# First stage of a hybrid token mixer: modulation as plain fp32 products, scale applied as a row, positions added by DMA

## Chip, cores and metric

One core of one Trainium2 chip runs the whole program. The metric is the device time of one execution in microseconds; the median of three runs stands for a kernel.

## What is computed

The reference is one layer of a diffusion backbone: 2048 latent tokens and 256 context tokens, 1024 wide. What matters here is its front part and the residual stream:

```python
x = x + grid_pos_embed(ROWS)                  # (2048, 1024): 512 columns by grid row, 512 by grid column
c_act, cctx_act = silu(c), silu(c_ctx)
mod_lat = c_act @ ada_w + ada_b               # six pieces of 1024: sh1, sc1, g1, sh2, sc2, g2
mod_ctx = cctx_act @ ada_w + ada_b
h_ctx = rmsnorm(ctx, norm1_g) * (1 + csc1) + csh1
h_lat = rmsnorm(x, norm1_g) * (1 + sc1) + sh1
y_ctx, states = token_mixers(h_ctx @ w_in, ...)
y_lat, _ = token_mixers(h_lat @ w_in, ..., states)
x = x + g1 * (y_lat @ w_out)
x = x + g2 * (relu(modulate(rmsnorm(x, norm2_g), sh2, sc2) @ w1) ** 2 @ w2)
return rmsnorm(x, final_g)
```

## The kernel before

Large products are made in three fp32r passes: an operand is split into a rounded part ("h" or "hi") and the rest ("l" or "lo"), and hi·h, hi·l and lo·h are added in psum. TensorE's instructions stand in the order in which the program issues them; those of the other engines are ordered by a scheduler, by priorities, and each engine and each DMA queue then works in order.

The first stage is the part that matters.

- **Modulation** (lines 264 to 298). The first 2048 columns of `ada_w` come in 32 tiles `aw` of 128x512, through eight buffers, on SP's queue. ScalarE rounds each to `awh`, VectorE or GpSimd subtracts to `awl`, and TensorE adds two products per tile into four psum banks `mps`; the stationary side is `csp`, silu(c) and silu(c_ctx) split in the same way. The four rows are copied out, transposed into a column layout (line 287) and become `mT` (shift and scale with the bias) and `sc1` (gain times one plus scale), one value per channel and per stream.
- **norm_in** (240 to 254), for each tile of 128 tokens: `xt` (four buffers) is loaded; for a latent tile `add_pos` loads `prow` in two DMAs and GpSimd adds `prow` and `posc` to the two halves of `xt` (237, 238). ScalarE squares with an accumulator (251), `rstd_of` makes the reciprocal root on ScalarE and VectorE with one Newton step (215 to 225), and VectorE scales `xt` by it (253). Four tiles are prepared ahead (two of context, two latent ones), and later ones two tiles ahead.
- **modulate** (436 to 452): TensorE transposes `xt` in two halves of four 128x128 blocks into psum `tp0` (four buffers). Each block is multiplied by `sc1` and shifted by `mT`, five of eight on VectorE (448), three on ScalarE (450), into `hy` (three buffers). ScalarE rounds to `hTh` (451), VectorE (first half) or GpSimd (second half) subtracts to `hTl` (452).
- **first(g)** (427): when a token group is complete, two column blocks of `w_in` are multiplied with it; these products are fed in between the tiles, 2.7 us of them a tile (`Filler`). Groups are 0 (context, 256 tokens, two tiles) and 1 to 4 (512 latent tokens, four tiles each). Line 462 then needs the products of group 4, and the other projections follow without a gap.

The output projection (`w_out`, 1253) loads x again, tile by tile, and calls `add_pos` a second time before the residual sum. `load_wo` brings a second copy of `posc` for it.

```python
r0, r1 = rstd_of(nrm, ss, 1, D, "n1")
nc.vector.tensor_scalar(xt, xt, r0, r1, op0=ALU.mult, op1=ALU.mult)
...
if k < 2 + hf:
    nc.vector.tensor_scalar(y[:, k, :], tp[:, k, :], sc1[:, kk, s:s + 1], mT[:, kk, s:s + 1], op0=ALU.mult, op1=ALU.add)
else:
    nc.scalar.activation(y[:, k, :], tp[:, k, :], AF.Identity, scale=sc1[:, kk, s:s + 1], bias=mT[:, kk, s:s + 1])
```

## Time and profile before

| | |
|---|---|
| median of three runs | 2805.06 us (2803.17 to 2809.77) |
| profiled execution | 2810.26 us |
| its span | 2808.50 us |
| mean granted clock of TensorE | 0.958 |
| busy share of the span | TensorE 91%, VectorE 63%, ScalarE 41%, GpSimd 35% |
| DMA, mean over the span | 178 GB/s |

The profile is of one execution. PE is TensorE (PEld its weight loads, which overlap the products), DVE VectorE, ACT ScalarE, POOL GpSimd, SP SyncE; a letter q behind a name is the engine's instruction queue, where DMAs are issued. Times of rows count from the start of the span. In a row of the order of time "x8" means that eight like instructions are merged, and the bracket gives the engine's idle time before them with what ended it. Shares over the whole span mix stages with different limits; the first stage is some 138 us of it.

### The profile page before, as it was taken

Reading aid. Unit: us, or ns where it says so; the run is one execution under the profiler, and the core shown is the slowest. Engines: PE = TensorE matmul, PEld = TensorE weight load, DVE = VectorE, ACT = ScalarE, POOL = GpSimd, SP = SyncE. Lnnn points to the kernel's source line nnn. Section 1 sums busy time; section 2 is a strip of 40 time slices with the busy share of each in tenths; the row PEclk is TensorE's granted clock in tenths of the full one; section 3 lists DMA queues with packets and bytes.
Section 4 is the critical chain, followed back from the end, with each engine's and each line's share of the span. In section 5 each row is a group of like instructions: output and inputs, shape, how many; then the busy total and the mean of one; then the engine's idle time right before and its main releaser. Section 6 shows DMA issues by size and latency. Waiting matters only on the chain. (4 is left out here: it accounts for less than half of the span.)

```text
span 2808.5 us, 36451 instructions
## 1 busy us (share of the span) xinstructions
PE 2559.5 (91%) x12239; PEld 2084.5 (74%) x12239; DVE 1775.4 (63%) x3041; ACT 1162.4 (41%) x2039; POOL 986.9 (35%) x868
## 2 busy tenths in 40 slices
PE   6798889899998888889996999989997999999997
PEld 3576667788887667777775888778885888878876
DVE  7955476156647886646657777766664275565576
ACT  6745421233335656433324444544444333222343
POOL 5724411245444443324444333333431222222211
PEclk7999989999999999889998999999998999999999
DMA  7443355666556665856754776655556576776564
GB/s 221 144 132 109 96 160 161 159 158 161 152 158 171 187 180 168 277 169 207 230 175 127 200 213 200 175 162 156 144 154 203 165 250 196 233 248 211 156 196 150
DMA packets 496455, 499.44 MB, mean 178 GB/s; under 512 B 88578, under 2 KB 371932, under 8 KB 496268
## 3 DMA queue, kind: packets, MB, share of 16 engines
q1 hardware_dynamic: 470316, 469.77, 55.6%
q10 hardware_dynamic: 20480, 15.73, 1.7%
q0 software_dynamic: 5472, 11.60, 1.5%
q8 instruction: 97, 1.59, 0.2%
q14 instruction: 90, 0.74, 0.1%
HBM read 345.27 MB, written 151.72 MB: 177 GB/s over the span
## 5 line engine op out<-in xcount | busy, mean ns | idle before, releaser
L365 PE MATMUL pp<-hTh,whi 128*128 128x512 f32 (+1 forms) x1048 | 435.1, 415 | 15.7 <-DVE evt L505 12.1
L367 PE MATMUL pp<-hTh,wlo 128*128 128x512 f32 (+1 forms) x1048 | 409.2, 390 | 2.2 <-POOL wlo L313 2.0
L366 PE MATMUL pp<-hTl,whi 128*128 128x512 f32 (+1 forms) x1048 | 407.3, 389 | 0.2 <-DVE hTl L452 0.2
L1714 PE MATMUL yps<-bh,ah 128*128 128x512 f32 x896 | 351.9, 393 | 17.5 <-ACT bh L1629 17.1
L1716 PE MATMUL yps<-bh,al 128*128 128x512 f32 x896 | 352.4, 393 | 12.0 <-DVE al L1421 11.2
L1715 PE MATMUL yps<-bl,ah 128*128 128x512 f32 x896 | 351.4, 392 | 0.5 <-DVE bl L1421 0.5
L1421 POOL TENSOR_TENSOR al<-ar,ah 128x1024 fp32r<-128x1024 f32 x56 | 141.8, 2531 | 504.3 <-ACT ah L1643 504.3
L1643 ACT CAST ah<-ar 128x1024 fp32r<-128x1024 f32 x112 | 117.9, 1053 | 359.0 <-PE yps L1715 313.3
L365 PEld LDWEIGHTS pp<-hTh,whi 128*128 128x128 f32 x1048 | 205.7, 196 | 53.4 <-DVE evt L505 14.0
L367 PEld LDWEIGHTS pp<-hTh,wlo 128*128 128x128 f32 x1048 | 204.0, 195 | 45.8 <-POOL wlo L313 3.7
L366 PEld LDWEIGHTS pp<-hTl,whi 128*128 128x128 f32 x1048 | 205.7, 196 | 35.5 <-issue 1.9
L1714 PEld LDWEIGHTS yps<-bh,ah 128*128 128x128 f32 x896 | 170.0, 190 | 53.5 <-ACT bh L1629 17.6
L1716 PEld LDWEIGHTS yps<-bh,al 128*128 128x128 f32 x896 | 169.9, 190 | 50.6 <-DVE al L1421 13.2
L1715 PEld LDWEIGHTS yps<-bl,ah 128*128 128x128 f32 x896 | 170.0, 190 | 36.6 <-DVE bl L1421 1.0
L1424 POOL TENSOR_TENSOR uz<-tz 128x512 f32<-128x512 f32 x32 | 50.3, 1572 | 387.1 <-ACT whi L1455 273.5
L1464 PE MATMUL accy<-th,wlo 128*128 128x512 f32 x384 | 151.2, 394 | 1.3 <-DVE wlo L1421 1.3
L1462 PE MATMUL accy<-th,whi 128*128 128x512 f32 x384 | 150.5, 392 | 1.7 <-DVE tz L1424 1.7
L1463 PE MATMUL accy<-tl,whi 128*128 128x512 f32 x384 | 150.3, 391 | 0.0
L1421 DVE TENSOR_TENSOR wlo<-wab,whi 128x512 fp32r<-128x512 f32 x128 | 117.1, 916 | 42.8 <-ACT whi L1455 42.8
L1421 DVE TENSOR_TENSOR wlo<-ws,whi 128x512 fp32r<-128x512 f32 x96 | 84.4, 879 | 92.0 <-ACT whi L1455 91.8
L1455 ACT CAST whi<-wab 128x512 fp32r<-128x512 f32 x128 | 79.2, 619 | 135.6 <-PE accy L1463 56.4
L1627 DVE TENSOR_TENSOR braw<-braw 128x1024 f32<-128x1024 f32 x56 | 75.0, 1339 | 72.5 <-DMA braw<-in_mlp_w_dram 69.6
(384 smaller groups left out, 5959.0 us busy)
## 6 DMA issues: line engine op xcount, KB each, us to landing
uD<-uz SPq DMA_DIRECT2D x224, 256.0 KB
ar<-uD SPq DMA_DIRECT2D x112, 512.0 KB
braw<-in_mlp_w_dram SPq DMA_DIRECT2D x112, 512.0 KB
wab<-in_mlp_w_dram SPq DMA_DIRECT2D x64, 512.0 KB
maw<-in_ada_w_dram SPq DMA_DIRECT2D x64, 256.0 KB
wraw<-in_w_in_dram SPq DMA_DIRECT2D x54, 256.0 KB
rb<-rD SPq DMA_DIRECT2D x96, 128.0 KB
aw<-in_ada_w_dram SPq DMA_DIRECT2D x32, 256.0 KB
```

The source lines that it names most:

```text
L365: nc.tensor.matmul(acc[:, 0:n], hi, hTh[g][:, k, :], start=k == 0, stop=False)
L366: nc.tensor.matmul(acc[:, 0:n], hi, hTl[g][:, k, :], start=False, stop=False)
L367: nc.tensor.matmul(acc[:, 0:n], lo, hTh[g][:, k, :], start=False, stop=k == KC - 1)
L1421: eng.tensor_tensor(o, a, b, op=ALU.subtract)
L1455: nc.scalar.copy(hi, w)
L1462: nc.tensor.matmul(acc, hi[:, k, :], T2[i][0][:, k, :], start=first and k == 0, stop=False, skip_group_check=True)
L1463: nc.tensor.matmul(acc, hi[:, k, :], T2[i][1][:, k, :], start=False, stop=False, skip_group_check=True)
L1464: nc.tensor.matmul(acc, lo[:, k, :], T2[i][0][:, k, :], start=False, stop=k == 3, skip_group_check=True)
L1643: nc.scalar.copy(hi, r_)
L1714: nc.tensor.matmul(acc, ah[:, p_, :], bh, start=p_ == 0, stop=False)
L1715: nc.tensor.matmul(acc, ah[:, p_, :], bl, start=False, stop=False)
L1716: nc.tensor.matmul(acc, al[:, p_, :], bh, start=False, stop=p_ == 7)
```

## The change

The modulation is no longer split: TensorE multiplies `cact` (silu of both streams, fp32) with the raw `aw` tile, one product instead of two, with no cast and no subtraction (line 265 now).

For latent tiles the scale is applied before the transposes. The two scale rows of the modulation are turned into one row of 1024 values (one plus bias plus scale, times the gain, lines 283 and 284), two products with a row of ones spread it over the partitions (289) and the copies of these make `scB`. `norm_in` then leaves a latent `xt` unscaled and hands on the reciprocal root `r0`; `modulate` makes `xt * r0 * scB` in one instruction (441) before the transposes, and one sum per half adds the shift behind them (449). Context tiles keep the old way. All `hTl` subtractions go to GpSimd (458).

The positions are a full 2048x1024 table in DRAM; `add_pos` is now one DMA per tile on GpSimd's queue that adds the table's rows to `xt` in place, in the first stage (16 of 512 KB) and in the output projection (16). `posc`, `prow`, the 64 loads of `prow` and the 64 GpSimd sums are gone.

```diff
-    csp = const.tile([P, KC, 4], F32R, name="csp")
...
-    def add_pos(pool, posc, i, xt, bufs=2):
-        prow = pool.tile([P, 512], F32, name="prow", bufs=bufs)
-        for hf in range(2):
-            nc.sync.dma_start(prow[64 * hf:64 * hf + 64, :], I["pos_r"][2 * i + hf:2 * i + hf + 1, :].to_broadcast([64, 512]))
-        nc.gpsimd.tensor_tensor(xt[:, 0:512], xt[:, 0:512], prow, op=ALU.add)
-        nc.gpsimd.tensor_tensor(xt[:, 512:1024], xt[:, 512:1024], posc, op=ALU.add)
+    def add_pos(i, xt):
+        nc.gpsimd.dma_start(xt, I["pos"][i * P:(i + 1) * P, :], accum_op=ALU.add)
...
-        nc.vector.tensor_scalar(xt, xt, r0, r1, op0=ALU.mult, op1=ALU.mult)
-        return xt
+        if g == 0:
+            nc.vector.tensor_scalar(xt, xt, r0, r1, op0=ALU.mult, op1=ALU.mult)
+            return xt, None
+        nc.vector.tensor_tensor(r0, r0, r1, op=ALU.mult)
+        return xt, r0
...
-                ah = adp.tile([P, 512], F32R, name="awh", bufs=3)
-                al = adp.tile([P, 512], F32R, name="awl", bufs=3)
-                nc.scalar.copy(ah, aw)
-                (nc.gpsimd if i % 5 in (0, 2) else nc.vector).tensor_tensor(al, aw, ah.bitcast(F32), op=ALU.subtract)
-            nc.tensor.matmul(mps[j][0:4, :], csp[:, k, :], ah, start=k == 0, stop=False)
-            nc.tensor.matmul(mps[j][0:2, :], csp[:, k, 0:2], al, start=False, stop=k == KC - 1)
+            nc.tensor.matmul(mps[j][0:2, :], cact[:, k, :], aw, start=k == 0, stop=k == KC - 1)
...
-    for j in range(4):
-        mrow = adp.tile([4, 512], F32, name="mrow", bufs=2)
-        (nc.vector.tensor_copy if j % 2 else nc.scalar.copy)(mrow, mps[j][0:4, :])
+    for j in (2, 3, 0, 1):
+        mrow = adp.tile([2, 512], F32, name="mrow", bufs=4)
+        (nc.vector.tensor_copy if j % 2 else nc.scalar.copy)(mrow, mps[j][0:2, :])
+        if j >= 2:
+            js = slice(512 * j - D, 512 * j - D + 512)
+            nc.vector.scalar_tensor_tensor(arow[:, js], arow[:, js], 1.0, mrow[0:1, :], op0=ALU.add, op1=ALU.add)
+            nc.vector.tensor_tensor(arow[:, js], arow[:, js], nrow[:, js], op=ALU.mult)
...
+    for hf in range(2):
+        sb = pp()
+        nc.tensor.matmul(sb, ones1, arow[:, 512 * hf:512 * hf + 512])
+        (nc.vector.tensor_copy if hf else nc.scalar.copy)(scB[:, 512 * hf:512 * hf + 512], sb)
...
+        if g:
+            nc.vector.scalar_tensor_tensor(xt, xt, rs, scB, op0=ALU.mult, op1=ALU.mult)
...
+            if g:
+                nc.vector.tensor_tensor(y, tp, mT[:, ks, 0:1].to_broadcast([P, 4, P]), op=ALU.add)
...
-            (nc.gpsimd if hf else nc.vector).tensor_tensor(hTl[g][:, ks, ts_], y, hTh[g][:, ks, ts_].bitcast(F32), op=ALU.subtract)
+            nc.gpsimd.tensor_tensor(hTl[g][:, ks, ts_], y, hTh[g][:, ks, ts_].bitcast(F32), op=ALU.subtract)
```

The change also moves instructions. On TensorE, behind the modulation (`mrow` are the modulation's rows, `tp` the transposed halves, the first two those of context tile 0), before:

```order
L279 MATMUL tr<-ident,pr 128x128
L287 MATMUL tr<-ident,mrow 128x4 x16
L444 MATMUL tp_551<-ident,xt 128x128 x4
L444 MATMUL tp_563<-ident,xt 128x128 x4
```

and now:

```order
L267 MATMUL tr<-ident,pr 128x128
L286 MATMUL tr<-ident,mrow 128x2 x16
L289 MATMUL pp<-row_287,row_288 128x512 x2
L447 MATMUL tp_394<-ident,xt 128x128 x4
L447 MATMUL tp_406<-ident,xt 128x128 x4
```

The two spreading products (`row_287` is the row of scales, `row_288` the ones) stand between the modulation's transposes and the context tiles.

On VectorE, at the same place (`ss_162` and `ss_181` are the squares of latent tiles 0 and 1, `tp0_551` to `tp0_587` the context halves), before:

```order
L448 TENSOR_SCALAR hy_552<-tp0_551,sc1_494,mT_491 128x128
L225 TENSOR_SCALAR n1t_151<-n1t_151 128x1
L448 TENSOR_SCALAR hy_552<-tp0_551,sc1_494,mT_491 128x128
L253 TENSOR_SCALAR xt_141<-xt_141,n1r_146,n1t_151 128x1024
L448 TENSOR_SCALAR hy_564<-tp0_563,sc1_494,mT_491 128x128 x3
L452 TENSOR_TENSOR hTl0_87<-hy_552,hTh0_86 128x4x128
L448 TENSOR_SCALAR hy_576<-tp0_575,sc1_494,mT_491 128x128 x2
L448 TENSOR_SCALAR hy_588<-tp0_587,sc1_494,mT_491 128x128 x3
L218 TENSOR_SCALAR n1v_168<-ss_162 128x1
```

and now (`ss_153` and `ss_168` are the squares of latent tiles 0 and 1, `row10241_287` the row of scales):

```order
L216 TENSOR_SCALAR n1v_159<-ss_153 128x1
L283 SCALAR_TENSOR_TENSOR row10241_287<-row10241_287,mrow_294 1x512
L219 SCALAR_TENSOR_TENSOR n1t_161<-n1r_156,n1v_159 128x1
L284 TENSOR_TENSOR row10241_287<-row10241_287,row10240_286 1x512
L223 TENSOR_SCALAR n1t_161<-n1t_161 128x1
L283 SCALAR_TENSOR_TENSOR row10241_287<-row10241_287,mrow_302 1x512
L216 TENSOR_SCALAR n1v_174<-ss_168 128x1
L247 TENSOR_TENSOR n1r_156<-n1r_156,n1t_161 128x1
L284 TENSOR_TENSOR row10241_287<-row10241_287,row10240_286 1x512
```

The variances of latent tiles 0 and 1 now stand ahead of the last instruction that makes the row of scales, and the context tiles' pieces come later.

Those pieces stand in the next stretch of VectorE (`tp0_394` to `tp0_431` belong to the context tiles, `xt_150`, `xt_165` and `xt_442` are latent tiles 0, 1 and 2):

```order
L290 COPY scB_293<-pp_325 128x512
L454 TENSOR_SCALAR hy_395<-tp0_394,sc1_337,mT_335 128x128 x2
L454 TENSOR_SCALAR hy_407<-tp0_406,sc1_337,mT_335 128x128 x3
L454 TENSOR_SCALAR hy_419<-tp0_418,sc1_337,mT_335 128x128 x2
L441 SCALAR_TENSOR_TENSOR xt_150<-xt_150,n1r_156,scB_293 128x1024
L441 SCALAR_TENSOR_TENSOR xt_165<-xt_165,n1r_171,scB_293 128x1024
L216 TENSOR_SCALAR n1v_451<-ss_445 128x1
L219 SCALAR_TENSOR_TENSOR n1t_453<-n1r_448,n1v_451 128x1
L223 TENSOR_SCALAR n1t_453<-n1t_453 128x1
L247 TENSOR_TENSOR n1r_448<-n1r_448,n1t_453 128x1
L441 SCALAR_TENSOR_TENSOR xt_442<-xt_442,n1r_448,scB_293 128x1024
L454 TENSOR_SCALAR hy_431<-tp0_430,sc1_337,mT_335 128x128 x3
```

The last half of the second context tile comes behind the variance and the scaling of latent tile 2, whose buffer `xt` is that of context tile 0.

## Rows read from the trace of the kernel before

**Rows 1.** Stretches of the span: length, then each engine's busy us (instructions), clock, DMA, GB/s.

```profile
100.00:130.00 30.00, 23.73 (x127) 19.30 (x126) 28.73 (x65) 24.35 (x60) 24.59 (x20) 1.00 0.43 139
140.00:160.00 20.00, 20.00 (x101) 16.86 (x100) 8.57 (x17) 6.78 (x12) 6.35 (x12) 1.00 0.55 152
```

**Rows 2.** Order of time, TensorE (start, us, engine, line, operation): transposes; last group's first product.

```profile
38.48 1.94 PE L444 MATMUL tp<-ident,xt 128*128 128x128 f32 x8 [2.54 <-DVE n1v L218]
...
64.09 1.94 PE L444 MATMUL tp<-ident,xt 128*128 128x128 f32 x8 [3.56 <-DVE xt L253]
...
130.84 1.07 PE L444 MATMUL tp<-ident,xt 128*128 128x128 f32 x8
...
137.62 0.50 PE L365 MATMUL pp<-hTh,whi 128*128 128x512 f32 x1 [1.52 <-ACT hTh L451]
```

**Rows 3.** Order of time, modulation: weight loads, first cast, two products, the last product.

```profile
1.92 24.66 SPq L271 DMA_DIRECT2D aw<-in_ada_w_dram  x32
...
4.63 1.27 ACT L274 CAST awh<-aw 128x512 fp32r<-128x512 f32 x2 [0.85 <-DMA aw<-in_ada_w_dram]
...
10.69 0.63 PE L277 MATMUL m<-awl,csp 128*2 128x512 f32 x1
...
12.50 0.39 PE L276 MATMUL m<-awh,csp 128*4 128x512 f32 x1
...
32.75 0.40 PE L277 MATMUL m<-awl,csp 128*2 128x512 f32 x1
```

**Rows 4.** Order of time, weight loads (PEld) of the mixer's fp32 gate products.

```profile
169.36 3.06 PEld L574 LDWEIGHTS qk<-xc,gw 128*128 128x128 f32 x8 [3.73 <-issue]
...
234.02 0.19 PEld L574 LDWEIGHTS qk<-xc,gw 128*128 128x128 f32 x1 [0.24 <-issue]
234.45 0.19 PEld L574 LDWEIGHTS qk<-xc,gw 128*128 128x128 f32 x1 [0.24 <-issue]
```

**Rows 5.** Order of time: issue of the first x loads, first use of one.

```profile
32.58 0.90 SPq L247 DMA_DIRECT2D xt<-in_x_dram  x2
...
38.03 2.71 POOL L238 TENSOR_TENSOR xt<-xt,posc 128x512 f32<-128x512 f32 x2 [5.89 <-DMA xt<-in_x_dram]
```

**Rows 6.** GpSimd's DMAs by tile: landing of lr (192 KB); issue and landing of bU (256 KB).

```profile
DMA to landing us min/median/max: 2.4/3.5/5.1
...
L1182 POOL DMA_DIRECT2D bU<-vbD x12: 754/772/795, 1103.0 to 1245.8; - x12
...
DMA to landing us min/median/max: 4.0/5.5/7.4
```

**Rows 7.** Groups of ScalarE, 33 to 150 us (busy us, mean ns of one | idle before).

```profile
L251 ACT ACTIVATE junk<-xt 128x1024 bf16<-128x1024 f32 x18 | 19.0, 1056 | 6.8 <-POOL xt L237 6.7
```

**Rows 8.** Stretch 45 to 57 us, instructions on whi alone (the first weights).

```profile
45.00:57.00 12.00, 2.13 (x7) 1.96 (x8) 5.20 (x8) 0.00 (x0) 0.00 (x0) 0.50 0.79 216
```

**Rows 9.** Groups of VectorE, 33 to 150 us.

```profile
L448 DVE TENSOR_SCALAR hy<-tp,sc,mT 128x128 f32<-128x128 f32 x90 | 32.6, 402 | 3.2 <-PE tp L444 2.2
L253 DVE TENSOR_SCALAR xt<-xt,n1r,n1t 128x1024 f32<-128x1024 f32 x18 | 22.1, 1229 | 0.8 <-DVE n1t L225 0.3
L452 DVE TENSOR_TENSOR hTl<-hy,hTh 128x512 fp32r<-128x512 f32 x18 | 21.1, 1170 | 1.3 <-ACT hTh L451 1.2
L221 DVE SCALAR_TENSOR_TENSOR n1t<-n1r,n1v 128x1 f32<-128x1 f32 x18 | 9.5, 528 | 1.6 <-ACT n1r L216 1.3
```

**Rows 10.** Groups of VectorE, whole span: a sum from psum, a sum of two SBUF tiles.

```profile
L1249 DVE TENSOR_TENSOR yg<-tr,ga 128x512 f32<-128x512 f32 x26 | 17.8, 684 | 0.3 <-PE tr L1247 0.3
...
L1627 DVE TENSOR_TENSOR braw<-braw 128x1024 f32<-128x1024 f32 x56 | 75.0, 1339 | 72.5 <-DMA braw<-in_mlp_w_dram 69.6 <-issue 2.3
```

**Rows 11.** Groups of GpSimd, 33 to 150 us.

```profile
L452 POOL TENSOR_TENSOR hTl<-hy,hTh 128x512 fp32r<-128x512 f32 x18 | 25.7, 1428 | 23.5 <-ACT hTh L451 14.5 <-DVE hy L448 6.0 <-issue 2.8
```

**Rows 12.** Waits, 1190 to 1480 us (total, times, longest).

```profile
PE pp L1266 <- POOL yl L1251: 6.8, 9, 1.5
```

**Rows 13.** Order of time, VectorE: two casts of the first weights.

```profile
52.41 1.83 DVE L312 CAST whi<-wraw 128x512 fp32r<-128x512 f32 x2
```

More of the change, by code (lines that the diff above doesn't have):

```diff
@@ L50, in consts @@
     pos_c = np.concatenate([np.sin(ac), np.cos(ac)], -1).astype(np.float32)
-    pos_c = np.concatenate([pos_c, pos_c], 0)
+    pos = np.concatenate([np.repeat(pos_r, GRID_W, 0), np.tile(pos_c, (rows, 1))], 1)
+    pos = np.ascontiguousarray(pos.astype(np.float32))
     s = np.arange(P)[:, None]
@@ L247, in norm_in @@
             nc.sync.dma_start(xt, x[i * P:(i + 1) * P, :])
-            add_pos(nrm, posc, i, xt)
+            add_pos(i, xt)
         ss = nrm.tile([P, 1], F32, name="ss", bufs=3)
@@ L456, in body @@
             xts[tiles[i + 2]] = norm_in(*tiles[i + 2])
-        modulate(g, j, xts.pop((g, j)))
+        modulate(g, j, *xts.pop((g, j)))
         if g and j == 1:
@@ L1215, in load_wo @@
                 yield
-        wo["pos"] = op_.tile([P, 512], F32, name="posc2")
-        nc.sync.dma_start(wo["pos"], I["pos_c"])
+        wo["ready"] = True
     def y_in(i):
@@ L1258, in w_out @@
             nc.sync.dma_start(x2s[i], x[i * P:(i + 1) * P, :])
-            add_pos(wo["op"], wo["pos"], i, x2s[i], 1)
+            add_pos(i, x2s[i])
         x2 = x2s[i]
@@ L1329, in out_proj @@
         yield from until(0)
-        while "pos" not in wo:
+        while "ready" not in wo:
             yield None
```

37 lines of the change are left out of this document (18 added, 19 removed).

## The prediction

> **What bounds the kernel now.** I read the table of stretches first. Behind the first stage TensorE is dense: 20.00 us busy of the 20 us from 140 to 160 [rows 1]. So the stage delays everything by as much as it lasts, and each us that it ends earlier or later is taken as one us of the kernel. I set the stage's end where the first product of the last token group starts, 137.62 us, which waits for ScalarE's last hTh [rows 2].
>
> The order of time shows three parts. Until 33.15 us the modulation is computed [rows 3]. Then come the context tiles (transposes from 38.48) and the first latent ones; the transposes of latent tile 2 (counted from 0) start at 64.09 and those of tile 15 at 130.84 [rows 2], so 13 tiles take 66.75 us, 5.13 each. In that steady part, from 100 to 130 (5.85 tiles), VectorE is busy 28.73 of 30 us, GpSimd 24.59, ScalarE 24.35, TensorE 23.73 at full granted clock [rows 1]. VectorE sets the pace with 4.9 us a tile, but the others stand close: 4.20, 4.16 and 4.06. Little can be won before the next one binds.
>
> **The modulation.** Removed are 32 ScalarE casts, 32 subtractions and one of two products a tile. What is left is a plain fp32 product of 128x512 for each of 32 weight tiles. The gate products of the mixer are such products: each shows as two loads and two passes, 0.43 us from load to load at 2.4 GHz [rows 4], so 0.86 a product; at 1.2 GHz the eight loads of products half as wide take 3.06 us, so 1.53 for a whole one. The small products of before take 0.63 us at 10.69 and 0.39 at 12.50 [rows 3]: the first stands for 1.2 GHz, the second for 2.4. The first weight tile is there at 4.63 [rows 3]. With 32 products at 0.86 the end is 32.2, with the slow rate until 11.1 it is 35.0; I take 34.5 against 33.15. TensorE, now the slower side, frees the eight weight buffers: the last load goes out after product 24, at 27.6, against 26.6 (1.92+24.66 [rows 3]). Everything behind it on SP's queue is about 1 us later, less the posc and prow loads that are gone.
>
> **The start of the tiles.** Here the change adds waits. VectorE's row of scales now has, ahead of its last multiply, the variance of latent tile 1; TensorE's two broadcast products wait for that multiply, and the context transposes are queued behind them, as the order in the section on the change shows. So the context tiles wait for latent tile 1's positions to have been added by DMA.
> - The x loads: before, issued at 32.58, the first was used at 38.03, when it landed [rows 5]. Now 38.5, the second 40.0.
> - The adding DMA, 512 KB issued by GpSimd: no row shows one. GpSimd's plain DMAs land 3.5 us after issue (192 KB, 2.4 to 5.1) and 5.5 (256 KB, 4.0 to 7.4) [rows 6]. The lower bound is 3.3, the fastest 192 KB row plus the missing 320 KB at the weights' rate (8.4 MB in 24.66 us, 340 GB/s); the upper is 10, the slowest 256 KB row plus 0.8 for the other half and 1.6 for reading what it adds to, rounded up. I take 5.0, the fast row plus 1.0 us of data and 1.6 for that second reading, nearest to the 5.5 for half the size. Landed: 43.5 and 45.0.
> - The square (1.06 [rows 7], with its accumulator 1.25), the variance (0.15) and the multiply (0.7) end at 47.1. Two fp32 broadcasts at 1.2 GHz, TensorE having idled, take 3.1: 50.2. Two tiles of context transposes at 1.94 [rows 2]: 54.2.
> - VectorE first makes the eight operands of the first weights, 5.20 us [rows 8], to 52.8, then half of scB, seven context pieces at 0.40 [rows 9] and two scalings of a latent tile, to 59.0.
> - Then it stands at tile 2's variance. That tile's buffer is free at 52.3; load 3.5, adding DMA 5.0, square 1.25, rest 1.3: 63.4, scaling done 64.7. Only then comes the last context half, and with it the psum buffer for tile 1's last half, ahead of 30 products of 256 columns (6.4 us). The transposes of tile 2 start at 73.3: **9.2 us later than before.**
>
> **The steady part.** VectorE loses, a tile, five affine pieces of 0.402, the scaling of 1.229 and the subtraction of 1.170 [rows 9]. It gains a scaling by a row, with two inputs from SBUF, a 128x1 product and two sums from psum. The sums cost 0.684 [rows 10]. The scaling's bounds are 1.25, what the square takes for the same elements, and 2.3, the 1.339 of a 128x1024 sum of two SBUF tiles [rows 10], stretched as the subtraction is to 1.170 from the 0.684 that a sum of its size takes; I take 1.5, near the 1.339, since GpSimd reads less than before. With the small ones (0.53 [rows 9], twice 0.15, 0.35 for the new one) and 0.34 of evacuations: 4.4 us. By the same sum of durations the tile of before has 5.56, of which 4.9 show as busy, since short ones overlap; so 3.9 to 4.4. GpSimd loses the two position sums and takes over the other subtraction: two at 1.43 [rows 11], 0.35 of memsets, and the issue of the DMA (a 256 KB one 0.77 [rows 6]; I take 1.0): 4.2 us, with waits for x in between. The row-wise loop of one buffer of four (load 3.5, DMA 5.0, square to scaling 4, transposes 1) is 13.5 us, 3.4 a tile, and does not bind. ScalarE only loses work. TensorE's 4.06 is the floor. I take **4.3 us a tile** between 4.06 and 5.2 (VectorE with the stretched scaling).
>
> **The sum.** VectorE has the sums of tiles 0 and 1 behind it at 68.7 and the scaling of tile 3 at 72.5. Left are the sums of tiles 2 and 3 (2.8) and 12 tiles at 4.3 (51.6): 126.9; idle time as in 100 to 130 (1.27 of 30) adds 2.3, the last cast 0.6: 129.8. That is 7.8 us before 137.62. In the output projection the 16 pairs of position sums go and 16 adding DMAs come. They lie beside TensorE's work: all its waits for GpSimd's yl are 6.8 us [rows 12], and the DMA waits for x where the sum waited. I take 0, with bounds of 2 us less and 4 more. The profiled run took 2810.26 us, of which the span is 2808.50; it lies 5.2 above the median of 2805.06. The sum makes 2802.5 of it, and **2797** of the median.
>
> On GpSimd's DMAs two rules of the Trainium skill speak. The page "DMA: Bandwidth & Descriptors" (Anatomy of one DMA, SWDGE path) fits about 2.0 us plus the bytes at 436 GB/s, an estimate of 3.2 us for these; the rows' 5.5 for 256 KB lie above it, and the short rival is that case. "SBUF — State Buffer" (Who interferes with whom) says that a VectorE copy, cast or scalar operation in its two-port mode keeps GpSimd from writing descriptors; the weight casts stand where the adding DMAs of tiles 0 to 2 are issued, and by one such cast pair (1.83 us [rows 13]) the sum would be 2799 instead of 2797. No row of before has such a DMA beside such a cast.
>
> **The rivals.**
> - **A short landing.** With 3.3 us, each of the two waits of the start is 1.7 shorter, and with TensorE's floor of 4.06 the stage ends at 123: 14 us saved, 2791. For it: the fast end of [rows 6]. Against it: x is added, not only written, while the small pieces of the first weights still move.
> - **No difference.** VectorE's scaling collides with GpSimd's two subtractions and a tile costs 4.8 to 5.1: 12 tiles take 6 to 10 us more than forecast and pay back no more than the start lost, 2803 to 2807. For it: the subtraction's 1.170 against 0.684 shows what such a collision costs.
> - **Slower, the landing chain.** The DMA's landing L enters the start twice and the loop of four tiles once, (8.5+L)/4 a tile, which passes 4.3 from 8.7 us on. With L=9 the stage ends at 138.7, with 10 at 143.7; from there the kernel is slower by 0.2%, and 11 gives about 2816. For it: 7.4 us already for 256 KB without adding. Against it: the medians.
> - **The fp32 products don't get the fast clock.** 32 at 1.53 end at 54 instead of 34.5, 19 us later, about 2816. Against it: TensorE is less idle than in the loop of before, which did get it.
>
> **How the numbers follow.** Forecast, 6 to 10 us saved: 0.31. Short landing: 0.17. No difference: 0.28. Landing chain 0.20, slow clock 0.04. A measurement of this kernel can tell about 0.2%, 5.6 us, from no change: faster 0.48, same 0.28, slower 0.24. The range leaves out a twentieth below and some 0.12 above: 2788 is the short landing with 2 us from the projection, 2812 a landing a little over 10 us.
>
> **What would show it.** One product row a weight tile, and the last about 34.5; the context transposes at 50 to 52 behind the two broadcasts, with VectorE waiting for ScalarE's square ahead of them; tile 2's transposes near 73; GpSimd's DMA rows with a landing near 5 us; then 4.3 us from tile to tile and the granted clock full from 80 on. I am wrong if tile 2 comes before 66 or after 80, if tiles still need 5 us, or if TensorE behind the stage waits where it did not.

## The result, and the profile after

The changed kernel took **2825.93 us** (median of four runs; 2822.88 to 2828.76), the kernel before on the same chip 2805.60 (2803.17 to 2809.77). The ratio, here and below estimated from all runs and not from the two medians, is 1.0070, 95% interval 1.0051 to 1.0090: **slower by 0.7%**, where 2797 had been forecast. The profiled run took 2828.76 us, its span is 2827.0 (before 2810.26 and 2808.5), so 18.5 us of span are to be found.

Stretches of the kernel after; columns as in [rows 1]:

```profile
100.00:130.00 30.00, 22.38 (x110) 18.73 (x111) 21.57 (x40) 14.86 (x33) 17.71 (x15) 0.83 0.85 187
```

Against [rows 1] every engine has become *less* busy: VectorE 21.57 of 30 us instead of 28.73, GpSimd 17.71 instead of 24.59. Yet fewer tiles get through. What rose is the DMA share, from 0.43 to 0.85. No engine sets the pace any more.

TensorE in the order of time, after; this answers to [rows 2] and the last of [rows 3] (the first row covers 13 products and ends at 35.28):

```profile
29.54 5.74 PE L265 MATMUL m<-aw,cact 128*2 128x512 f32 x13
...
36.34 1.13 PE L286 MATMUL tr<-ident,mrow 2*128 2x2 f32 x16 [0.80 <-DVE prm L268]
48.62 2.07 PE L289 MATMUL pp<-row,row 1*128 1x512 f32 x2 [11.15 <-DVE n1t L223]
51.79 2.07 PE L289 MATMUL pp<-row,row 1*128 1x512 f32 x2 [1.10 <-DVE row L284]
53.80 1.54 PE L447 MATMUL tp<-ident,xt 128*128 128x128 f32 x6
...
76.50 1.03 PE L447 MATMUL tp<-ident,xt 128*128 128x128 f32 x8
...
150.37 1.03 PE L447 MATMUL tp<-ident,xt 128*128 128x128 f32 x8
```

The modulation ends where it was forecast. Then TensorE stands for 11.15 us in front of the broadcasts of the scale row, the context transposes start at 53.80 (before 38.48, forecast 50.2), tile 2's at 76.50 (before 64.09), tile 15's at 150.37 (before 130.84). Thirteen tiles take 73.87 us, **5.68 each**; before 5.13, forecast 4.3.

The adding DMAs of the first stage, GpSimd's tile xt (durations of the issue in ns, then landing in us):

```profile
L229 POOL DMA_DIRECT2D xt<-in_pos_dram x16: 801/856/1207, 39.7 to 138.6; - x16
...
DMA to landing us min/median/max: 5.2/6.6/9.1
```

They land after 6.6 us in the median, where 5.0 was taken. ScalarE's groups, 33 to 165 us, show who waits for them (beside [rows 7]):

```profile
L242 ACT ACTIVATE junk<-xt 128x1024 bf16<-128x1024 f32 x18 | 19.0, 1056 | 42.4 <-DMA xt<-in_pos_dram 41.9 <-DMA xt<-in_ctx_dram 0.5
```

VectorE's groups, 80 to 140 us, beside [rows 9] and [rows 10]:

```profile
L441 DVE SCALAR_TENSOR_TENSOR xt<-xt,n1r,scB 128x1024 f32<-128x1024 f32 x11 | 17.1, 1556 | 0.4
L449 DVE TENSOR_TENSOR hy<-tp,mT 128x512 f32<-128x512 f32 x21 | 14.2, 686 | 1.0 <-PE tp L447 0.7
L247 DVE TENSOR_TENSOR n1r<-n1r,n1t 128x1 f32<-128x1 f32 x10 | 7.7, 773 | 0.3
L219 DVE SCALAR_TENSOR_TENSOR n1t<-n1r,n1v 128x1 f32<-128x1 f32 x10 | 6.7, 666 | 1.8 <-ACT n1r L214 1.7
```

The scaling (1556) and the sums (686) are near the 1.5 and 0.684 us assumed. Two products of a *single column* cost 773 and 666 ns.

**Where the 18.5 us are.** Six landmarks of both traces, in us of the span; each is the start of an instruction, the end excepted. Their differences are not evenly spread, and one of them is negative:

| landmark | before | after | difference |
|---|---|---|---|
| ScalarE's last cast hTh of the stage | 138.30 | 155.12 | +16.8 |
| first qk product of L1155 (after: L1161), in the mixer's last part | 1116.8 | 1133.2 | +16.4 |
| first product of the output projection (yl) | 1238.7 | 1243.2 | +4.5 |
| first product of the MLP's accy | 1492.4 | 1498.2 | +5.8 |
| last product of accy | 2144.6 | 2159.7 | +15.1 |
| end | 2808.5 | 2827.0 | +18.5 |

So there are three effects: the first stage loses 17, the way into the output projection gives 12 of them back, and the MLP, where no line of the change is at work, loses 9 in accy (from +5.8 to +15.1) and 3 more behind it.

### The profile page after: what moved, and what is told of

Same layout as the page of the kernel before. It is cut to its first block, busy times and chain, and to the rows that moved or that the text cites. A ratio compares the mean times of both kernels' runs of the same rounds, so it can differ in the third digit from the quotient of the medians.

```text
span 2827.0 us, 36023 instructions
## 1 busy us (share of the span) xinstructions
PE 2589.2 (92%) x12243; PEld 2088.2 (74%) x12243; DVE 1739.7 (62%) x2975; ACT 1128.6 (40%) x1960; POOL 930.9 (33%) x841
```

## The experiments

Every ratio is to the kernel before on the same chip, whose median was between 2807.5 and 2809.5; the changed kernel itself was timed beside the 2805.60 above and not again. "A tile" is a thirteenth of the time from tile 2's transposes to tile 15's. It comes from one profiled run of each kernel, and kernels whose stage is the same differ in it: 5.13, 5.23 and 5.12 (before, e6, e17), 5.68 and 5.85 (after, e5). So 0.2 us a tile are not read as an effect.

### 1 to 4. The parts by themselves

e1 leaves the positions out of the first stage. e2 adds a fifth buffer. e3 keeps the new row of scales but the old position sums. e4 is the kernel before with the adding DMAs alone.

```diff
 e1                add_pos(i, xt)                      ->  (left out, in the first stage)
 e2    xt = nrm.tile(..., bufs=4); norm_in of tile i+2 ->  bufs=5; norm_in of tile i+3
 e3    add_pos by DMA  ->  prow, posc and two GpSimd sums; one of the two hTl subtractions on VectorE
 e4    before.py: prow, posc and the sums -> nc.gpsimd.dma_start(xt, I["pos"][...], accum_op=ALU.add)
```

> Leaves out: the positions in the first stage (the tiles are normalised without them; the output projection still adds them by DMA). Theory A (the row-wise loop of four buffers, made long by the adding DMA and by the queues that it stands in, sets 5.68 us a tile): the 13 tiles from tile 2 to tile 15 take 53 to 58 us instead of 73.87, tile 2 starts its transposes at 64 to 68 instead of 76.50, the stage's last hTh cast comes at 122 to 130 instead of 155.12, and the kernel takes about 2795 to 2802 us. Theory B (the DMA engines, 0.80 to 0.85 busy from 100 to 140, are full): the same time here, but with a DMA share under 0.5. Theory C (the fp32 modulation, the scaling by a row or the collision of VectorE and GpSimd cost it): tiles still need over 5 us and the kernel stays above 2815 us.

> The changed kernel with five buffers for the row tiles instead of four, and the look-ahead one tile deeper. Theory A (a loop of buffers): 4 x 5.68 = 22.7 us shared by five is 4.5 us a tile, at most 4.9; the 13 tiles take 59 to 64 us, the last hTh cast comes at 138 to 147, the kernel takes 2811 to 2818 us. Theory B (DMA engines full): 5.4 us a tile or more, DMA share still at 0.80 to 0.85, and the time within 4 us of 2826. Theory C: no difference either, but with VectorE or GpSimd busy over 0.9.

> The changed kernel with the positions back as before (GpSimd's two sums a tile, in the stage and in the output projection) and the subtractions shared again by VectorE and GpSimd; fp32 modulation and the scaling by a row stay. Theories A and B: tiles cost about 5.0 us, tile 2's transposes come at 64 to 68, the last hTh cast at 130 to 140, the kernel takes 2798 to 2808 us. Theory C: it stays slower than 2815 us.

> The kernel before with one part of the change alone: positions added by the accumulating DMAs, in the stage and in the output projection. Theories A and B: over 5.5 us a tile, tile 2's transposes at 70 or later, the last hTh cast at 148 to 158 instead of 138.30, the kernel takes 2817 to 2830 us. Theory C: 2800 to 2808 us. If the later parts lose time in this run too (the products from 1500 to 2150 us took 10 us longer in the profile of the changed kernel, at the same granted clock of 1.00), the adding DMAs or what they move in memory belong to it; if only in runs with the fp32 modulation, they don't.

| run | median us | ratio (95%) | context transposes | tile 2 | a tile | last cast |
|---|---|---|---|---|---|---|
| before, after | | 1; 1.0070 | 38.48; 53.80 | 64.09; 76.50 | 5.13; 5.68 | 138.30; 155.12 |
| e1 | 2805.01 | 0.9989 (0.9977 to 1.0002) | 47.33 | 64.81 | 4.79 | 132.60 |
| e2 | 2826.50 | 1.0063 (1.0045 to 1.0081) | 52.24 | 78.81 | 5.22 | 150.12 |
| e3 | 2843.29 | 1.0131 (1.0106 to 1.0155) | 55.65 | 76.70 | 6.33 | 162.09 |
| e4 | 2797.02 | 0.9958 (0.9941 to 0.9974) | 38.99 | 67.27 | 5.09 | 139.72 |

Without the adding DMAs a tile takes 4.79 us (e1), tile 2 comes at 64.81 and the stage ends at 132.60. So in the changed form the adds of the first stage cost 22.5 us (155.12 against 132.60), 11.7 of them by tile 2 and the rest behind it, and without them the stage would be 5.7 us shorter than before (138.30). The stretch of e1 from 100 to 120 us shows what then binds:

```profile
100.00:120.00 20.00, 15.67 (x81) 11.82 (x80) 19.66 (x30) 12.32 (x28) 12.05 (x11) 1.00 0.31 107
```

The same stretch with the fifth buffer (e2):

```profile
100.00:120.00 20.00, 16.63 (x87) 13.12 (x86) 16.05 (x30) 11.45 (x26) 11.79 (x11) 1.00 0.95 237
```

In e1 VectorE is busy 19.66 of 20 us with the DMA share at 0.31. So the row-wise form alone needs 4.8 us of VectorE, not 4.4. In e2 no engine is full, and the DMA engines stand at 0.95 in this stretch (0.84 from 80 to 130): a fifth buffer shortens a tile to 5.22, but the start is later and the total is as slow as the change.

e4 says that the same adds in the *old* form of the stage cost 1.4 us (139.72 against 138.30), nothing a tile (5.09 against 5.13), and that the kernel is *faster* by 0.4%. VectorE no longer sets that pace: it is busy 16.58 of 20 us in e4 from 100 to 120, where before has 19.25. e3 says that the old sums are worse still in the new form: with them and one subtraction on GpSimd a tile takes 6.33. The two theories that blamed the adds alone expected a slower stage of e4 and 5.0 us a tile in e3; both missed. Put together, the adds are slow only in the row-wise form (5.68 with them, 4.79 without), and that form is slow with the old sums as well (e3, at a DMA share of about 0.4).

### 5 to 8. The MLP's loss, the start, and the buffers again

In the MLP the products are the same, and so is the clock. Stretch 1900 to 2100 us, before:

```profile
1900.00:2100.00 200.00, 200.00 (x876) 164.09 (x875) 126.29 (x169) 91.67 (x156) 75.97 (x50) 1.00 0.55 154
```

And after:

```profile
1900.00:2100.00 200.00, 200.00 (x859) 161.13 (x858) 123.48 (x163) 89.45 (x152) 77.83 (x52) 1.00 0.52 148
```

TensorE is never idle in either, at granted clock 1.00, but gets through 859 products instead of 876 (1.9% fewer). The change removes csp, 128 bytes a partition at the low end of memory, and all tiles behind it, the MLP's operands too, lie 128 bytes lower. e5 and e6 test the place alone:

```diff
 e5 (after)    + held = const.tile([P, KC, 4], F32, name="held")     # where csp was, otherwise unused
 e6 (before)   - csp = const.tile(...)   + csp = adp.tile(...)         # same work; what follows lies 128 bytes lower
 e7 (e5)       scale row and its broadcasts ahead of all; the squares of x0 and x1 behind the first weights' splits
 e8 (e4)       bufs=5, norm_in of tile i+3
```

> The changed kernel with a tile of the size of csp (128 bytes a partition) held in its old place, so that all tiles behind it stand where they stood before the change. Theory D (places: without csp, hTh, hTl and the MLP's th and tl stand 128 bytes lower, and TensorE's products over them come slower: 859 products in 1900 to 2100 us in the four runs without csp, 875 and 876 in the two with it): 875 products in that stretch, the MLP's first products from the first to the last in 652 us instead of 661, the output projection's in 230 instead of 235, the stage unchanged, and the kernel at 2808 to 2814 us instead of 2826. Against D (the slower products come from the row scaling, the modulation or the chip): 859 again, and 2820 us or more.

> The kernel before, computing the same in the same order, with csp taken from the modulation's own pool instead of the constants, which moves what stands behind it 128 bytes lower, as the change does. Theory D: 859 products in a dense stretch of 200 us of the MLP, its first products in 661 us instead of 652, the kernel at 2817 to 2824 us instead of 2806. Against D: 2803 to 2810 us.

> The changed kernel with csp's place held, and with the start reordered: the row of scales has priority, and the squares of latent tiles 0 and 1 are made to follow the first weights' splits (by one 1x1 copy each into the tile that the square writes), so that neither the context tiles nor the weights stand behind a wait for positions. Theory E (the start's loss is VectorE's row of scales and weights standing behind the variances of latent tiles 0 and 1): the context transposes at 40 to 44 instead of 53.80, tile 2's at 66 to 71 instead of 76.50, the stage ends 5 to 10 us earlier than in the kernel with the place alone, the kernel at 2800 to 2806 us. Against E (the landings of tiles 2 and 3 set it): tile 2 still at 75 or later and within 3 us of the kernel with the place alone.

> The kernel before with the adding DMAs as its only change, and five row tiles instead of four with the look-ahead one deeper. Theory A (a loop of buffers with the landing in it): 4.81 us a tile with four buffers falls to 4.0 to 4.5, the stage ends 3 to 9 us earlier, the kernel at 2788 to 2794 us instead of 2797. Against A (the engines set 4.81): the same time as with four, 2797 within 3.

| run | median us | ratio (95%) | context transposes | tile 2 | a tile | last cast | accy, first to last |
|---|---|---|---|---|---|---|---|
| before, after | | 1; 1.0070 | 38.48; 53.80 | 64.09; 76.50 | 5.13; 5.68 | 138.30; 155.12 | 652.2; 661.5 |
| e5 | 2817.04 | 1.0033 (1.0017 to 1.0049) | 52.24 | 75.08 | 5.85 | 155.76 | 652.1 |
| e6 | 2813.87 | 1.0026 (1.0012 to 1.0040) | 39.08 | 65.15 | 5.23 | 139.45 | 662.3 |
| e7 | 2810.39 | 1.0010 (0.9998 to 1.0022) | 45.90 | 71.11 | 5.66 | 149.46 | 652.4 |
| e8 | 2796.79 | 0.9959 (0.9941 to 0.9977) | 37.92 | 67.20 | 5.17 | 139.53 | 653.1 |

The place counts, from both sides. With 128 bytes of nothing in csp's stead (e5) the stage stays as slow as the change's (155.76), accy is back at 652.1 and the ratio falls from 1.0070 to 1.0033, about 10 us. Moving csp away in the kernel before (e6) costs 0.26%, and accy takes 662.3. The stretch of e5:

```profile
1900.00:2100.00 200.00, 200.00 (x875) 164.09 (x875) 128.90 (x169) 93.31 (x158) 80.73 (x53) 1.00 0.53 150
```

And of e6:

```profile
1900.00:2100.00 200.00, 200.00 (x859) 160.29 (x858) 125.58 (x164) 91.34 (x155) 79.46 (x53) 1.00 0.52 147
```

The other traces agree with one exception. All five kernels without csp's 128 bytes (after, e1, e2, e3, e6) show 859 products in this stretch, and fourteen of the fifteen that have them 875 or 876. The fifteenth is e9 (below), which has them and moves no tile against e7:

```profile
1900.00:2100.00 200.00, 200.00 (x858) 162.00 (x858) 123.75 (x165) 90.02 (x153) 75.81 (x50) 1.00 0.53 149
```

Its accy runs at the faster pace up to 1810 us and at the slower one from there, 658.4 us in all. So the place is not the only thing that decides this pace.

e7 undoes a part of the start's mechanism: the broadcasts no longer stand behind the tiles' variances, the context transposes come at 45.90 instead of 52.24, tile 2's at 71.11 instead of 75.08, the stage ends 6.3 us earlier and the kernel is 6.6 us faster than e5 (2810.39 against 2817.04; the intervals just overlap). Tile 2 is still 7.0 later than before, and the steady part's loss remains, at 5.66 us a tile. A fifth buffer in the old form (e8) gives nothing, where 4.0 to 4.5 us a tile had been expected.

### 9 to 16. What holds a tile at 5.7 us

Left were collisions of VectorE and GpSimd, GpSimd's queue, and the DMAs themselves.

```diff
 e9  (e7)  - scalar_tensor_tensor(t, r0, r0, v, mult, mult)   + tensor_scalar(t, r0, r0, v, mult, mult)
           - tensor_tensor(r0, r0, r1, mult)                  + tensor_scalar(r0, r0, r1, None, mult)
 e10 (e9)  one of a tile's two hTl subtractions back on VectorE       e12: and five buffers
 e13 (e9)  both subtractions on VectorE                               e15: and five buffers
 e11 (e4)  the one-tensor form of the first product
 e14 (e4)  both subtractions on VectorE                               e16: and one-tensor form, five buffers
```

> The kernel with place and start mended, and VectorE's two 128x1 products of the normalisation written with one tensor and per-partition factors instead of two tensors (the same numbers come out). Theory F (VectorE's two-input forms wait for GpSimd's running subtraction: 0.69 and 0.61 us in the mean for products that take 0.22 and 0.16 alone, up to 2.75, and three such waits a tile lengthen the way from square to scaling): both products at 0.15 to 0.25 us, 5.66 us a tile falls to 4.9 to 5.4, the stage ends 3 to 9 us earlier, the kernel 3 to 9 us under the one with place and start mended. Against F (the landings and the queues set the tile): the products get short, the tile stays at 5.5 to 5.7, the time within 2 us.

> The kernel before it, with one of the two subtractions a tile given back to VectorE. Theory F: GpSimd runs half as long a tile, so the scaling by a row comes near its undisturbed 1.28 us (mean 1.65 before), and GpSimd issues its DMAs sooner; 4.7 to 5.0 us a tile, the stage another 3 to 8 us earlier. Against F (VectorE's own work sets the pace): VectorE at over 0.95 and no gain or a loss, as its 0.7 a tile more would give 9 us.

> The kernel before with two changes: positions by adding DMAs, and the 128x1 product of the normalisation with one tensor. Theory F: the product falls from 0.45 to 0.2 us and the stage ends 0 to 4 us earlier, the kernel at 0.994 to 0.996 of the one before, at or a little under the adding DMAs alone (0.9958). Against: no difference to 0.9958.

> The kernel with place, start, one-tensor products and shared subtractions mended, and five row tiles instead of four. Theory A (the landings in the loop of buffers bind the row-scaled form): 4.2 to 4.6 us a tile, the stage ends at or before 138.30 us, the kernel at 0.993 to 0.996 of the one before. Against A: no gain over the same kernel with four.

> The kernel with place, start and one-tensor products mended, and both subtractions a tile on VectorE, so that GpSimd has nothing in the steady part but the adding DMAs and a few memsets. Theory G (a ring of in-order queues: square ahead of the casts on ScalarE, casts ahead of the subtractions, subtractions ahead of the next adding DMA on GpSimd): 5.75 us a tile falls to 4.6 to 5.0, the stage ends 8 to 14 us earlier, at 136 to 142 us. Theory B (DMA engines): not under 4.7 us a tile, DMA share over 0.9. Against G: 5.5 or more, stage end at 148 or later.

> The kernel before with adding DMAs, and both subtractions a tile on VectorE. Theory G: issues of the adding DMAs come when x has landed; a gain of 2 to 6 us in the stage over the 139.72 us of the adding DMAs alone. Theory B: 4.7 to 4.9 us a tile as there (4.81), DMA share over 0.9, no gain. VectorE takes 0.69 a tile more and stays under 0.9.

> The kernel with both subtractions on VectorE in the row-scaled form, and five row tiles. Theory G: with the ring cut, the loop of buffers is next: 0.2 to 0.6 us a tile less than with four. Theory B: 4.7 to 4.9 us a tile with four and with five. Against both: over 5.3.

> The kernel before with adding DMAs, both subtractions a tile on VectorE, the 128x1 product with one tensor, and five row tiles. Theory B: 4.7 to 4.9 us a tile, the stage ends at 136 to 140, the time at 0.995 to 0.997 of the one before. Against B: under 4.5 us a tile, the stage ends before 134, the time at 0.993 or less.

| run | median us | ratio (95%) | tile 2 | a tile | last cast |
|---|---|---|---|---|---|
| e9 | 2813.75 | 1.0006 (0.9988 to 1.0023) | 71.82 | 5.75 | 149.75 |
| e10 | 2811.71 | 1.0008 (0.9994 to 1.0022) | 73.69 | 6.10 | 155.70 |
| e11 | 2800.62 | 0.9970 (0.9956 to 0.9983) | 64.62 | 5.09 | 137.09 |
| e12 | 2812.44 | 1.0024 (1.0008 to 1.0039) | 76.12 | 5.70 | 153.23 |
| e13 | 2817.38 | 1.0025 (1.0012 to 1.0039) | 72.41 | 6.08 | 154.31 |
| e14 | 2807.15 | 0.9981 (0.9966 to 0.9997) | 63.65 | 5.55 | 143.34 |
| e15 | 2818.44 | 1.0029 (1.0016 to 1.0041) | 78.29 | 6.02 | 159.30 |
| e16 | 2810.66 | 0.9994 (0.9979 to 1.0008) | 65.36 | 6.07 | 150.04 |

None of them got a tile of the row-wise form with adding DMAs under e2's 5.22, nor one of the old form with them under 5.09. Most expectations missed: for e9, e10, e12, e13 and e15 a shorter tile had been forecast, and e14 and e16, where a gain or no loss was expected, took 5.55 and 6.07. Only e11's stage came as expected, 2.6 us earlier than e4's. e9 removes the collisions of the small products, as its VectorE groups show (80 to 140 us):

```profile
L221 DVE TENSOR_SCALAR n1t<-n1r,n1v 128x1 f32<-128x1 f32 x10 | 2.7, 270 | 4.0 <-ACT n1r L216 4.0
L255 DVE TENSOR_SCALAR n1r<-n1r,n1t 128x1 f32<-128x1 f32 x10 | 2.1, 210 | 0.2
```

From 666 and 773 ns they fall to 270 and 210; a tile still takes 5.75. So these collisions bind where VectorE is full, and not here. To see what does, one buffer's loop was followed from row to row. Tile 10 of the kernel after, rows of SP, GpSimd, ScalarE, VectorE and TensorE in the order of time:

```profile
101.43 4.01 SPq L238 DMA_DIRECT2D xt<-in_x_dram  x2
...
104.94 3.54 POOL L458 TENSOR_TENSOR hTl<-hy,hTh 128x512 fp32r<-128x512 f32 x2 [3.99 <-ACT hTh L457]
...
109.08 0.87 POOL L229 DMA_DIRECT2D xt<-in_pos_dram  x1 [0.59 <-PE tp L447]
...
114.56 1.06 ACT L242 ACTIVATE junk<-xt 128x1024 bf16<-128x1024 f32 x1 [2.88 <-DMA xt<-in_pos_dram]
...
121.99 0.15 DVE L216 TENSOR_SCALAR n1v<-ss 128x1 f32<-128x1 f32 x1 [1.62 <-ACT junk L242]
122.07 1.28 DVE L441 SCALAR_TENSOR_TENSOR xt<-xt,n1r,scB 128x1024 f32<-128x1024 f32 x1
...
125.00 1.03 PE L447 MATMUL tp<-ident,xt 128*128 128x128 f32 x8
```

The load is issued at 101.43, the adding DMA only at 109.08, behind GpSimd's subtractions; the square, which waits for it, at 114.56; the scaling at 122.07, behind the variance of tile *11*, for which VectorE had stood idle 1.62 us, since that tile's landing was late too; the transposes at 125.00. Means over tiles 6 to 15, in us, from start to start (the transposes to their end):

| run | buffer free to load | load to add issued | add to square | square to scaling | scaling to transposes | transposes | sum, per buffer |
|---|---|---|---|---|---|---|---|
| after | 0.4 | 7.8 | 6.8 | 5.2 | 2.2 | 1.2 | 23.7, 5.9 |
| e9 | 0.3 | 8.5 | 6.6 | 4.2 | 2.6 | 1.2 | 23.4, 5.9 |
| e13 | 0.4 | 5.7 | 6.8 | 6.8 | 4.0 | 1.2 | 25.0, 6.3 |
| e4 | 0.2 | 5.9 | 7.1 | 3.8 | 2.5 | 1.1 | 20.7, 5.2 |
| e2 (five) | 0.6 | 9.7 | 6.7 | 5.4 | 3.3 | 1.1 | 26.9, 5.4 |

The load goes out almost as soon as its buffer is free (first column), so the sum over the number of buffers has to come near the time of a tile whatever sets the pace, and it does, to within 0.25 us in all five. The table shows where a buffer's time goes; it doesn't show that the buffers bind. The test for that is a fifth buffer: were the loop of fixed length, a tile would fall from 5.68 to 4.5 us and from 5.09 to 4.1. It fell to 5.22 in the changed form (e2, whose loop took 3.2 us longer), by 0.4 in e12 (5.70 against e10's 6.10), and neither in e15 (6.02 against e13's 6.08) nor in the old form (e8, 5.17). So a fifth buffer is worth 0.5 us a tile at best, and the rest is something else.

The second column can be taken apart by the packets of the DMA trace. Counted off in their order, 128 packets of 4 KB make a load. In the kernel after, the last packet of a load ends 4.8 us after the load's issue (mean of tiles 6 to 15; 3.1 in e1, where no adds run beside it), and the add is issued 3.0 us after that. In e13, where GpSimd has no subtractions, the load takes the same 4.8 and the add follows after 0.9. So freeing GpSimd shortens the second column from 8.5 to 5.7, but lengthens the fourth from 4.2 to 6.8, where the subtractions now stand on VectorE among scalings.

The same packets give what the DMA engines have to do for a tile. Kernel after, 90 to 130 us (packets, MB, share of all 16 engines):

```profile
q0 software_dynamic: 1018, 3.71, 54.7%
q1 hardware_dynamic: 1163, 3.67, 30.4%
```

The first row is the adds: 21.9 us of all 16 engines for 3.71 MB, 3.1 us for each 512 KB. The second is nearly everything else, mostly the loads of x, and makes 1.7 us for each 512 KB. That is 4.8 us a tile, more than the 4.3 that had been forecast for the whole tile, and e4's packets give the same rates (56.2% and 29.4%). It makes 0.85 of the time at 5.68 us a tile, so the DMA engines are near full and not full.

One thing that differs between the two forms with adds is what VectorE waits for. Its waits for squares from 80 to 130 us (total, times, longest), after, e13 and e4:

```profile
DVE n1v L216 <- ACT junk L242: 8.6, 6, 2.2
DVE n1v L218 <- ACT junk L250: 11.0, 4, 3.6
DVE n1v L219 <- ACT junk L245: 2.6, 3, 1.5
```

In the changed form VectorE waits for a later tile's square with an earlier tile's scaling behind it, as at 121.99 above; in the old form it hardly waits. This is read from the traces; no run changes that order alone.

### 17 and 18. The part that pays

e17 is the kernel before with the adding DMAs in the output projection alone (the second copy of posc goes with the sums), so the first stage is the old one. e18 adds e9's one-tensor form of the first product of rstd_of.

```diff
 e17 (before)  - add_pos(wo["op"], wo["pos"], i, x2s[i], 1)
               + nc.gpsimd.dma_start(x2s[i], I["pos"][i * P:(i + 1) * P, :], accum_op=ALU.add)
 e18 (e17)     - nc.vector.scalar_tensor_tensor(t, r0, r0, v, op0=ALU.mult, op1=ALU.mult)
               + nc.vector.tensor_scalar(t, r0, r0, v, op0=ALU.mult, op1=ALU.mult)
```

> The kernel before with adding DMAs in the output projection alone; the first stage keeps its sums. Theory H (GpSimd's position sums, which wait for a late row of positions, stand ahead of the mixer's last transfers on its queue): from the mixer's first qk products at 1117 us to the projection's first 108 to 112 us instead of 122, the stage ends at 138 to 139 us, and the kernel is at 0.995 to 0.997 of the one before. Against H (the gain comes with the stage's DMAs): 0.999 to 1.001.

> The same, with the 128x1 product of the normalisation in its one-tensor form. If VectorE's waits for GpSimd lengthen the stage of before, where VectorE is 0.96 busy: the stage ends 1 to 4 us earlier than with the adding DMAs in the projection alone, the time 1 to 4 us less. If not: the same within 2 us.

| run | median us | ratio (95%) | last cast | qk to yl | yl, first to last |
|---|---|---|---|---|---|
| before | 2809.28 | 1 | 138.30 | 121.9 | 235.2 |
| e17 | 2799.27 | 0.9964 (0.9950 to 0.9978) | 139.90 | 110.0 | 228.3 |
| e18 | **2789.04** | **0.9943 (0.9922 to 0.9965)** | 133.37 | 110.8 | 228.1 |

(The landmarks of before are those of its shown profile.) e17 has the same 110.0 from qk to yl as the kernel after, so the gain comes from these DMAs. Its size is less certain than one pair of traces says: the three kernels with the old sums there have 121.9, 118.8 and 118.6 (before, e3, e6), the seventeen with adds 106.4 to 114.8, twelve of them between 109.4 and 110.8. The rows of before say how. In the order of time, first VectorE:

```profile
1188.78 3.32 DVE L1148 COPY bx<-bk 64x512 f32<-64x512 f32 x1
...
1202.22 2.23 DVE L1159 TENSOR_TENSOR lr<-lr,eye 128x512 f32<-128x512 f32 x1
1204.48 0.76 DVE L1148 COPY bx<-bk 64x512 f32<-64x512 f32 x2
```

GpSimd beside it:

```profile
1189.32 1.27 POOL L1214 TENSOR_TENSOR wol<-yg,woh 128x512 fp32r<-128x512 f32 x1
1190.54 1.27 POOL L238 TENSOR_TENSOR x<-x,posc 128x512 f32<-128x512 f32 x1
...
1202.61 1.27 POOL L238 TENSOR_TENSOR x<-x,posc 128x512 f32<-128x512 f32 x1
1207.80 1.27 POOL L237 TENSOR_TENSOR x<-x,prow 128x512 f32<-128x512 f32 x1 [3.91 <-DMA prow<-in_pos_r_dram]
```

And TensorE:

```profile
1192.36 3.62 PE L1155 MATMUL qk<-bx,bq 128*128 128x256 f32 x8 [4.41 <-DVE bx L1148]
...
1205.16 3.75 PE L1155 MATMUL qk<-bx,bq 128*128 128x256 f32 x8 [3.94 <-DVE bx L1148]
```

The copy of bx usually takes 0.42 us. This one takes 3.32, ends 0.3 us after GpSimd's position sum (1190.54 + 1.27), and TensorE waits 4.41 us for it. The second wait, 3.94 us, is for copies that stand behind a VectorE instruction of 2.23 us (1202.22; its like at 1192.13 took 0.69), again beside a position sum (1202.61). For the next x tile the sum comes late itself, 3.91 us behind its prow load. In e3 and e6, which keep these sums, the longest such copy takes 2.07 us and TensorE waits 3.2 us once for VectorE's bx. Waits for VectorE's bx make 8.4 us of TensorE's time between the two landmarks of before and none in e17, where the longest such copy is 1.15 us. After idle time the clock is low as well: the same 527 products are busy for 99.94 us at a mean granted clock of 0.85 before, for 92.65 at 0.92 in e17. So of the 11.9 us, 7.3 are products at a faster clock and 4.6 less idle time. That the lower clock comes of these waits is inferred.

The Trainium skill says in "SBUF — State Buffer", section "Who interferes with whom", that a VectorE copy in its two-port mode and GpSimd lock each other out of a shared port pair for whole instructions, and that two SBUF inputs on VectorE contend with GpSimd's reads. The trace agrees: 3.32 us instead of 0.42 beside two GpSimd instructions back to back, and in the stage a one-column product of 269 ns in the one-tensor form where the two-tensor form shows 526 (means of 18, e18 and e17).

e18 is the fastest of all, though its seven runs spread from 2786 to 2804 us. The one-tensor form pays there because VectorE is the bound of the old stage (28.45 and 28.56 of 30 us busy, from 100 to 130, in e18 and e17): a tile falls from 5.12 to 4.93, tile 2 comes at 63.72 instead of 65.83, and the stage ends 6.5 us earlier. The medians differ by 10.2 us, the ratios by 0.0021 or 6 us; in the profiled runs 6 us more arise in the MLP's last products (yps, 634.0 and 627.7 us long), which the edit doesn't touch. So 6 us is what is explained, more than the 1 to 4 expected, and the two intervals overlap. Beside the first stage's adding DMAs (e11 against e4) the form paid nothing that could be measured: 0.9970 against 0.9958.

## Why the prediction was wrong

The sign was wrong, and the time lies outside the range (2788 to 2812). Point by point:

- **The modulation**: right. Last product at 35.28 against 34.5, on the fast clock; the slow-clock rival fell.
- **The start**: the mechanism was right, the size not. The two broadcasts did wait for tile 1's landing and the context transposes for them. These were to start at 50.2 and end at 54.2; they started at 53.80 and ended at 57.5. Tile 2's transposes started at 76.50 against 73.3, so +12.4 instead of +9.2. The term that was mis-sized is the landing of 5.0 us: it measured 6.2 and 8.6 for the first two (issued 39.69 and 41.05, squares of 45.91 and 49.75), and the 3.6 us that the second took too long are about what the context transposes came late. e7, in which the broadcasts go first, brings back 4.0 us at tile 2; e1, which has no adds, brings back 11.7.
- **The steady part**: here the prediction failed, in two steps. The first is the loop: "The row-wise loop of one buffer of four ... is 13.5 us, 3.4 a tile, and does not bind." A buffer's round measured 23.7 us. The load of 3.5 became 7.8 until the add was issued: 4.8 for the load itself beside the adds and 3.0 in GpSimd's queue, where subtractions stand ahead. The DMA of 5.0 became 6.8. From the square to the end of the transposes 5 became 8.6, because each step stands in line behind another tile's. I had added durations where each step has a queue ahead of it, and e2 shows that a buffer more is worth 0.5 us a tile. The second is a bound that the sum doesn't have: it weighs VectorE, GpSimd, ScalarE, TensorE and the buffers, and puts the DMA engines at nothing. Load and add take 4.8 us of all 16 engines a tile, so at these rates the 4.3 was out of reach. The rival "Slower, the landing chain" named the same loop with (8.5+L)/4, but put all the risk into L: with the measured L of 6.8 it gives 3.8 us, not 5.7.
- **VectorE's 4.4 us a tile**: its large terms were right, 1556 ns for the scaling against 1.5 and 686 for the sum against 0.684. The small ones were not: the two one-column products, 0.53 and 0.35 us in my sum, took 0.67 and 0.77 beside GpSimd's subtractions, and e1 shows 4.79 a tile with VectorE full. Even with no positions to add the stage gains 5.7 us (132.60 against 138.30) and not 7.8, and that with tile 2 nearly as early as before (64.81 against 64.09). The rival "No difference" had this price of a tile. That e1's time is also the time of before (0.9989) is chance: its stage gains 5.7 us, and the place and the projection, which the rival didn't have, make up the rest.
- **The output projection**: taken as 0 with bounds of 2 us less and 4 more; it gave 12 us between these two traces, ahead of its own first product. I had looked for TensorE's waits for yl [rows 12] and not for what GpSimd's sums do to VectorE in the phase before. The x tiles are loaded and summed from 1184 on, some 55 us before their first product (1238.7).
- **Places**: not in the prediction at all. 128 bytes less in the constants cost about 10 us (e5) or 7 (e6).
- **By its own signs** the prediction is wrong as well: tiles still need more than 5 us. That the time lies only 14 us outside the range is luck: the projection's 12 and the MLP's 13 us, neither of them foreseen, nearly cancel.

By landmark: 12.4 at the start and 7.1 in the steady part, less 2.7 at the end of the stage, make 16.8. From there to the projection's first product 12.3 come back, 1.3 are lost in the projection, accy loses 9.3, and the rest of the MLP 3.4. That is 18.5. Shown by runs that change them alone are the adds' part in the stage (e1: 22.5 us, which the rest of the change reduces by 5.7), the place's part in accy (e5, e6) and the projection's approach (e17). e7 shows a part of the start.

**Open.** What makes up a tile's 5.68 us is settled in part: VectorE's own 4.8 (e1), the DMA engines' 4.8 and the buffers' 0.5 (e2) are measured, but no single one is full. That a tile's scaling stands behind the next tile's variance is read from the trace only; the other order was not tried. Why e14 and e16, in the old form, are slower a tile than e4 no run explains, nor why e3 is the slowest. The 3 us in yps, whose length lies between 627.7 and 635.8 in these runs, are not settled. Why the place of an operand matters to TensorE, and why e9 changes pace in the middle of accy, was not tried beyond the one shift of 128 bytes. The yl stretch itself went from 235.2 to 228 in e17 and e18, but 236.1 in e5 and 229.1 in e7, which no run explains.

## What to carry to other kernels

When a transfer is put between the load and the first use of a buffer, count it twice. In the buffer's round, add what stands *ahead of each step in its engine's queue* and not only the steps: here 23.7 us and not 13.5. And count it as work of the DMA engines, as for any other engine: here 4.8 us a tile, above the 4.3 that was forecast. A round that equals the buffers times the tile proves nothing by itself; one more buffer is the test. An accumulating DMA was cheap where the data are needed late, as in the output projection, and in the old form of the stage; it was dear in the form that has a later tile's variance ahead of an earlier tile's scaling. Look for VectorE instructions that take many times their usual time beside GpSimd work, small ones too, before and not only in the changed stage; and after an edit that removes a tile, compare the products per stretch somewhere that the edit does not touch.

## What the runs showed of the hardware that was not expected

- TensorE made 876 or 875 dense fp32r products of 128x512 in 200 us with accy's operands in the old place (before, e5) and 859 with them 128 bytes lower (after, e6), at granted clock 1.00 and with no idle time. The shortest product of accy shows 387 ns before and 392 after. e9 has the old place and 858.
- An adding DMA of 512 KB into on-chip memory landed after 5.2, 6.6 and 9.1 us (least, median, longest) in the first stage of the kernel after; the least of all runs is 5.1. On that path the Trainium skill ("DMA: Bandwidth & Descriptors", Anatomy of one DMA) would give an estimate of 3.2 us, which no run here came near. By its packets such a DMA takes 3.1 us of all 16 DMA engines, a plain load of the same size 1.7.
- A VectorE product of one column took 666 to 773 ns in the mean beside GpSimd's subtractions, up to 1.25 us in the rows of the loop above (L219 at 117.19), and 210 to 270 with the second operand as a per-partition scalar.
